# The low parts of 124 weight blocks: an accumulating transfer onto the negated rounded block instead of a VectorE difference

## The chip, the cores and the metric

The kernel runs on one core of one Trainium2 chip. The metric is device time in microseconds (us) of one execution on that core; lower is better. Engines are named as in the profile: PE is TensorE, DVE is VectorE, ACT is ScalarE, POOL is GpSimd, SP is SyncE, which issues the DMA transfers of the kernel before.

## The reference

One layer of a hybrid decoder is computed for 512 prompt tokens and 8 x 4 sample tokens, which share the weights. Cut to what matters here:

```
z   = rmsnorm(x) @ w_in                      # 1024 -> 9736: mixers a, b, c and the merge gates
y_a = (B * dwconv3(C * x_a)) @ w_out_a
y_b = silu(layernorm(dwconv31(...))) @ w_out_b
y_c = (sigmoid(o) * mlstm(q, k, v, ig, fg)) @ w_out_c      # 4 heads, chunks of 128
x  += (sig(g_a)*y_a + sig(g_b)*y_b + sig(g_c)*y_c) @ w_o
mk, mv = split(rmsnorm(mem) @ w_xkv)         # 256 memory tokens
x  += cross_attn(rmsnorm(x) @ w_xq, mk, mv) @ w_xo
x  += (silu(gate) * up) @ w_ffn_out          # gate, up = split(rmsnorm(x) @ w_ffn_in)
y   = rmsnorm(x)
```

All of it is float32, and every matrix product is wanted at nearly float32 accuracy.

## The kernel before

**Products in three passes.** Every operand of a product is held as two tiles: a high part, which is the float32 value rounded to the matmul format (fp32r), and a low part, which is the value minus its high part. A product is the sum of high x high, high x low and low x high. `PASSES` gives the order for each slice of 128 rows: the weight's high part with the activation's high part, then with its low part, and then the weight's low part with the activation's high part. With two halves of 272 tokens that is six matmuls for each slice; the weight's low part is first read by the fifth.

**Weight blocks.** PE's order is written by hand; the other engines' orders are made by a scheduler from the program's order and priorities. All weights are cut into blocks, and `order` is the list of them in the order in which PE uses them: `("in", j)` of `w_in`, `("v", ..)` and `("k", j)` of the memory's projection, `("oc"/"oa"/"ob", j)` of the mixers' output projections, `("o", j)`, `("xq", j)`, `("xo", j, half)`, `("fi", f, i)` of the first five feed-forward pairs, and others (`s..`, `fo`) later. A block is mostly 128 x 1024 numbers: eight slices, 48 matmuls of 272 columns, or 24 of 256 columns for the memory blocks. `oa`, `ob` and `xo` blocks are 128 x 512: 24 matmuls.

`w_emit` prepares a block: a DMA on SP's queue brings it into a raw tile `wr` (four of them), and `split` makes the two parts in a tile `w`: ACT writes the high part by a copy (`w<-wr` on ACT), then DVE writes raw minus high (`w<-wr,w` on DVE). There are **three** tiles `w` for all blocks. So the high part of a block can only be written when PE has ended with the block whose tile it takes; `wget` emits blocks two to four ahead. From then on the block has the time until PE comes to it.

**Stages.** Up to 46 us: the start, with the first two query blocks and two key blocks of head 0. 46 to 162 us: blocks of head 0 mixed with the sixteen memory blocks; here the block of output gate 0 spreads over 41 us and keeps one of the three `w` tiles, so the memory blocks turn over in two. 162 to 398 us: heads 1 to 3. 398 to 567 us: merge of mixer c and the inputs of mixer a, 1024-wide blocks one after the other. 567 to 712 us: the merges with `oa` and `ob`, where 1024-wide and 512-wide blocks alternate. 712 to 915 us: `o`, cross-attention with `xq` and `xo`. 915 to 983 us: the first five feed-forward pairs, two `fi` blocks each. After 983 us: the other pairs, which use another scheme (`s_emit`), and the final norm.

At the start POOL raises `small` (the mean squares of x) to the power -0.5 (`rms_pow`); PE's transposes in the middle of block `("in", 28)` wait for it.

Of the kernel before, what the change touches and what calls it, by code (L numbers as in the profile page):

```python
# [11 lines left out]
AF = mybir.ActivationFunctionType  # L12
# [23 lines left out]
def layer(ctx: ExitStack, tc: tile.TileContext, a):  # L36
    nc = tc.nc
# [27 lines left out]
    def nm(s):  # L65
        cnt[0] += 1
        return f"{s}_{cnt[0]}"
# [26 lines left out]
    def TTo(out, x, y, op):  # L94
        nc.vector.tensor_tensor(out=out, in0=x, in1=y, op=op)  # L95
# [7 lines left out]
    def STT(out, x, s, y, op0, op1):  # L103
        nc.vector.scalar_tensor_tensor(out=out, in0=x, scalar=s, in1=y, op0=op0, op1=op1)  # L104

    def ACT(out, x, f, **kw):
        nc.scalar.activation(out, x, f, **kw)  # L107
# [4 lines left out]
    def split(hi, lo, src, scale=None):  # L112
        if scale is None:
            ACT(hi, src, AF.Copy)
            TTo(lo, src, hi.bitcast(F32), ALU.subtract)
        else:
            ACT(hi, src, AF.Copy, scale=scale)
            STT(lo, src, scale, hi.bitcast(F32), ALU.mult, ALU.subtract)
# [4 lines left out]
    MULT, ADD, SUB, MAX, MIN = ALU.mult, ALU.add, ALU.subtract, ALU.max, ALU.min  # L123
# [22 lines left out]
    for h in range(NH):  # L146
        for base in (20, 28, 36, 44):
            for d in range(2):
                order += [("in", base + 2 * h + d)]
                if base == 44 and h == 0 or h == 1 and base < 36:  # L150
                    n = (1, 7)[d] if h == 0 else 2
# [36 lines left out]
    def w_emit(key, parts=1):  # L188

        if key[0][0] == "s":  # L190
            with tc.high_priority(PRIO):
                return s_emit(*key)
        if key[0] == "fo":
            return fo_emit(key)
        if key[0] == "v":
            src, n = a["w_v"][key[1], key[2]], 1024
        elif key[0] == "xo":
            n = 512
            src = a["w_xo"][key[1]][:, key[2] * n:(key[2] + 1) * n]
        elif key[0] == "fi":  # L200
            n = 1024
            src = a["w_fi"][key[1]][:, key[2] * n:(key[2] + 1) * n]
        else:
            src = a[src_of[key[0]]][key[1]]
            n = src.shape[-1]
        raw = sb.tile([P, 1024], F32, tag="wr", name=nm("wr"), bufs=4)
        w = sb.tile([P, 2, 1024], F32R, tag="w", name=nm("w"), bufs=3)
        wt[key] = w

        def part(i):  # L210
            c = slice(i * n // parts, (i + 1) * n // parts)
            with tc.high_priority(PRIO if parts == 1 and key not in (("in", 28), ("in", 29)) else 0):
                nc.sync.dma_start(out=raw[:, c], in_=src[:, c])
                split(w[:, 0, c], w[:, 1, c], raw[:, c])
        if parts == 1:
            part(0)
        return part

    def fo_emit(key):

        n = key[3] * P
        with tc.high_priority(PRIO):
            if n > 512:
                raw = sb.tile([P, 1024], F32, tag="wr", name=nm("wr"), bufs=4)
            else:
                raw = sb.tile([P, 512], F32, tag="sraw", name=nm("fr"), bufs=5)
            nc.sync.dma_start(out=raw[:, :n], in_=a["w_ffn_out"][key[1]][:, key[2] * P:key[2] * P + n])
            if n > 512:
                w = sb.tile([P, 2, 1024], F32R, tag="w", name=nm("w"), bufs=3)
            elif key in order[-6:]:  # L230
                w = act_t([P, 2, 512])
            else:
                w = sb.tile([P, 2, 512], F32R, tag="spair", name=nm("fw"), bufs=2)
            split(w[:, 0, :n], w[:, 1, :n], raw[:, :n])
        wt[key] = w
# [3 lines left out]
    def s_emit(part, f):  # L239

        if part == "sA":
            r = [sb.tile([P, 1024], F32, tag="wr", name=nm("wr"), bufs=4) for _ in range(2)]
            for i in range(2):
                nc.sync.dma_start(out=r[i], in_=a["w_fi"][f][:, i * 1024:(i + 1) * 1024])
            sraw_[f] = r
        r1, r2 = sraw_[f]
        if part in ("sA", "sC", "sE"):
            src = {"sA": r1[:, 0:512], "sC": r2[:, 0:512], "sE": r1[:, 512:]}[part]
            if f == NSTD and part != "sE":
                w = sb.tile([P, 2, 512], F32R, tag="spair", name=nm("fw"), bufs=2)  # L250
            else:
                w = act_t([P, 2, 512])
        else:
            w = sb.tile([P, 2, 1024], F32R, tag="w", name=nm("w"), bufs=3)
            if part == "sB":
                src = sb.tile([P, 1024], F32, tag="wr", name=nm("wr"), bufs=4)
                TTo(src.rearrange("p (a n) -> p a n", a=2), r1.rearrange("p (a n) -> p a n", a=2),
                    r2[:, 512:].rearrange("p (a n) -> p a n", a=1).to_broadcast([P, 2, 512]), ADD)
                TTo(r2[:, 512:], src[:, 512:], r1[:, 0:512], ADD)
            else:  # L260
                src = r2
                TTo(r2[:, 0:512], r2[:, 0:512], r2[:, 512:], ADD)
        split(w[:, 0, :], w[:, 1, :], src)
        wt[(part, f)] = w
# [800 lines left out]
    for c in range(4):  # L1065
# [13 lines left out]
        for j in range(3):  # L1079
            w = vec[:, V_AW + c * 3 + j:V_AW + c * 3 + j + 1]  # L1080
# [462 lines left out]
    parts = (slice(NP // 2, T), slice(0, NP // 2))  # L1543
# [183 lines left out]
```

## Time and profile before

| | |
|---|---|
| time, median of 3 runs (lowest to highest) | 1311.14 us (1310.72 to 1311.30) |
| the profiled execution's own time | 1310.35 us |
| its span, first to last instruction | 1308.3 us |
| PE busy | 1287.3 us, 98% of the span, 10160 matmuls |
| DVE busy | 887.5 us, 68% |
| ACT busy | 593.2 us, 45% |
| POOL busy | 40.9 us, 3% |
| DMA, mean share of 16 engines | 40.1% |

The profiled execution lies 0.8 us under the median, and 2.05 us of its time lie outside the span. Of the 1308.3 us PE is idle for 21.0. An engine that is not the one waited for may be idle, or busier, at no cost; what counts is which wait ends last in a stage.

### The profile page before, as it was taken

The page shows a single profiled execution, that of the slowest core. Times are in us where ns is not written, and L with a number is a line of the kernel's source. Part 1 is how long each engine was busy: PE and PEld are TensorE (multiplying, and loading weights), DVE is VectorE, ACT ScalarE, POOL GpSimd, SP SyncE. Part 2 cuts the span into 40 slices and gives each one's busy share as a digit, 9 for nine tenths or more (in the row PEclk, how much of TensorE's full clock was granted, in tenths as well). Part 3 has the DMA queues.
Part 4 walks back from the last instruction along what each step waited for, and adds up shares of the span by engine and source line. Part 5 has one row for each costly group of instructions (what it writes and reads, how often), then busy time and mean ns, then how long its engine had stood idle before and what let it go on. Part 6 is the DMA issues. An engine that isn't in the chain of part 4 may idle for free.

```text
span 1308.3 us, 24794 instructions
## 1 busy us (share of the span) xinstructions
PE 1287.3 (98%) x10160; PEld 1272.2 (97%) x10160; DVE 887.5 (68%) x1487; ACT 593.2 (45%) x1046; POOL 40.9 (3%) x117
## 2 busy tenths in 40 slices
PE   9899999999999999999999999999999999999997
PEld 9899999999999999999999999999999999999997
DVE  7955665655497859976444557886787667777746
ACT  6845545554433222226332446765544444444433
POOL 1000010010010000000000000000000000000000
PEclk9989999999999999999999999999999999999999
DMA  7355644434465333432334224664323323333212
GB/s 263 102 173 172 193 131 141 122 113 148 116 153 165 91 88 83 82 75 88 88 125 148 81 90 149 204 189 145 94 76 111 88 93 109 92 95 95 80 41 69
DMA packets 83265, 155.68 MB, mean 119 GB/s; under 512 B 25124, under 2 KB 33700, under 8 KB 83152
## 3 DMA queue, kind: packets, MB, share of 16 engines
q1 hardware_dynamic: 83152, 154.10, 40.1%
q8 instruction: 80, 1.31, 0.4%
q14 instruction: 33, 0.27, 0.1%
HBM read 137.54 MB, written 16.52 MB: 118 GB/s over the span
## 4 chain that ended last, share of the span: by engine, by line
PE 89%; DVE 5%; DMA 3%; issue 2%; ACT 2%; SPq 0%; POOL 0%; DVEq 0%; POOLq 0%; ACTq 0%
PE mm L110 60%; PE s L110 14%; PE sy L1475 8%; PE sz L1475 4%; PE sx L1475 2%; DVE f L95 1%; DMA out_sct<-ct 1%; DVE w L95 1%; DVE f L104 1%; ACT act L107 0%; DMA kr<-in_vc 0%; ACT w L107 0%; DMA f<-kscr 0%; DVE act L95 0%; DMA lt<-in_xT 0%
## 5 line engine op out<-in xcount | busy, mean ns | idle before, releaser
L110 PE MATMUL mm<-act,w 128*128 128x272 f32 x6336 | 837.8, 289 | 1.5 <-ACT f L107 0.9
L110 PEld LDWEIGHTS mm<-act,w 128*128 128x128 f32 x6336 | 809.5, 189 | 4.4 <-ACT f L107 1.1
L107 ACT ACTIVATE w<-wr 128x1024 fp32r<-128x1024 f32 (+2 forms) x202 | 196.6, 975 | 392.1 <-PE mm L110 228.9
L95 DVE TENSOR_TENSOR w<-wr,w 128x1024 fp32r<-128x1024 f32 (+2 forms) x202 | 225.5, 1117 | 144.3 <-ACT w L107 143.6
L104 DVE SCALAR_TENSOR_TENSOR f<-act,const,f 128x512 f32<-128x512 f32 (+1 forms) x136 | 96.5, 719 | 2.4
L95 DVE TENSOR_TENSOR lt<-mm,lt 128x544 f32<-128x544 f32 x56 | 40.4, 722 | 55.6 <-PE mm L110 55.4
L110 PE MATMUL mm<-act,fw 128*128 128x272 f32 x576 | 76.2, 288 | 0.0
L110 PEld LDWEIGHTS mm<-act,fw 128*128 128x128 f32 x576 | 73.9, 188 | 0.0
L107 ACT ACTIVATE act<-f 128x544 fp32r<-128x544 f32 (+3 forms) x75 | 44.3, 600 | 47.1 <-DVE f L95 40.8
L110 PE MATMUL s<-act,act 128*128 128x256 f32 (+4 forms) x408 | 62.9, 302 | 1.3 <-DVE act L95 0.8
L95 DVE TENSOR_TENSOR act<-f,act 128x544 fp32r<-128x544 f32 (+3 forms) x75 | 48.4, 653 | 22.1 <-ACT act L107 21.9
L95 DVE TENSOR_TENSOR f<-f,f 128x544 f32<-128x544 f32 (+4 forms) x78 | 51.3, 659 | 14.4 <-ACT f L107 13.1
L110 PEld LDWEIGHTS s<-act,act 128*128 128x128 f32 (+1 forms) x408 | 55.0, 184 | 4.4 <-DVE act L95 1.1
L1475 PE MATMUL sy<-bt,w 128*128 128x272 f32 x408 | 56.9, 288 | 0.6 <-ACT f L107 0.6
L1475 PEld LDWEIGHTS sy<-bt,w 128*128 128x128 f32 x408 | 53.4, 188 | 0.8 <-ACT f L107 0.8
L104 DVE SCALAR_TENSOR_TENSOR ct<-ct,wbc,s 128x258 f32<-128x258 f32 x64 | 28.7, 479 | 26.4 <-PE s L110 26.4
L107 ACT ACTIVATE f<-sy 128x272 f32<-128x272 f32 x51 | 19.8, 391 | 39.6 <-PE sy L1475 39.6
L95 DVE TENSOR_TENSOR wr<-wr,wr 128x1024 f32<-128x1024 f32 (+1 forms) x34 | 32.4, 954 | 5.4 <-DMA wr<-in_w_fi 4.9
L95 DVE TENSOR_TENSOR f<-mm,f 128x544 f32<-128x544 f32 (+1 forms) x29 | 20.7, 721 | 22.5 <-PE mm L110 20.4
L107 ACT ACTIVATE fw<-fr 128x512 fp32r<-128x512 f32 x26 | 16.4, 632 | 42.9 <-PE mm L110 39.0
L107 ACT ACTIVATE f<-mm 128x544 f32<-128x544 f32 (+1 forms) x50 | 30.6, 612 | 7.2 <-PE mm L110 7.0
L95 DVE TENSOR_TENSOR xpair<-kr,xpair 128x512 fp32r<-128x512 f32 x46 | 30.7, 682 | 3.5 <-ACT xpair L107 3.4
(238 smaller groups left out, 1406.3 us busy)
## 6 DMA issues: line engine op xcount, KB each, us to landing
wr<-in_w_in SPq DMA_DIRECT2D x74, 512.0 KB, 3.7
wr<-in_w_fi SPq DMA_DIRECT2D x44, 512.0 KB, 3.6
ct<-in_ctn SPq DMA_DIRECT2D x32, 258.0 KB, 3.1
out_sct<-ct SPq DMA_DIRECT2D x32, 258.0 KB, 3.8
kr<-in_ktc SPq DMA_DIRECT2D x32, 256.0 KB, 3.2
kr<-in_vc SPq DMA_DIRECT2D x32, 256.0 KB, 3.3
fr<-in_w_ffn_out SPq DMA_DIRECT2D x32, 256.0 KB, 2.7
lt<-in_xT SPq DMA_DIRECT2D x16, 272.0 KB, 3.9
```

The lines of the kernel that those rows point to most:

```text
L95: nc.vector.tensor_tensor(out=out, in0=x, in1=y, op=op)
L104: nc.vector.scalar_tensor_tensor(out=out, in0=x, scalar=s, in1=y, op0=op0, op1=op1)
L107: nc.scalar.activation(out, x, f, **kw)
L110: nc.tensor.matmul(out, lhsT=l, rhs=r, start=start, stop=stop)
L1475: nc.tensor.matmul(ps, lhsT=w[:, wi, c + k * P:c + (k + 1) * P], rhs=x(k, ai), start=first and k == 0 and n == 0, stop=k == 3 and n == 2, ...
```

## The change

For the 1024-wide blocks that `w_emit` loads whole (124 of them), ACT makes the high part as before, and then a second copy of the raw tile with scale -1 into the low half of `w`, which gives the negated rounded block. A DMA issued from POOL then reads the block a second time from memory and adds it onto that half, so that raw minus high stands there. DVE's difference is gone. The first two blocks (in two parts) and the 512-wide blocks keep `split`; so do the blocks that `fo_emit` and `s_emit` prepare.

```diff
@@ -211,7 +211,12 @@
             c = slice(i * n // parts, (i + 1) * n // parts)
             with tc.high_priority(PRIO if parts == 1 and key not in (("in", 28), ("in", 29)) else 0):
                 nc.sync.dma_start(out=raw[:, c], in_=src[:, c])
-                split(w[:, 0, c], w[:, 1, c], raw[:, c])
+                if parts == 1 and n == 1024:
+                    ACT(w[:, 0, c], raw[:, c], AF.Copy)
+                    ACT(w[:, 1, c], raw[:, c], AF.Copy, scale=-1.0)
+                    nc.gpsimd.dma_start(out=w[:, 1, c], in_=src[:, c], accum_op=ADD)
+                else:
+                    split(w[:, 0, c], w[:, 1, c], raw[:, c])
         if parts == 1:
             part(0)
         return part
```

PE's order and its instructions stay as they are. Lines after 219 stand five lines lower. Three places of the orders follow.

POOL from the rms of x on, before: `small_315` and `small_853` are the powers for x and for the memory, `f_98_675` a cleared tile of the gates, `km_..` a masked key of the sample tokens.

```order
L381 ISA
L381 TENSOR_TENSOR small_315<-small_314,const_67 128x5
L121 MEMSET f_98_675 68x544
L381 TENSOR_TENSOR small_853<-small_852,const_67 128x2
L874 TENSOR_SCALAR km_1424<-ks_1280,ph_157 96x256
```

The same place after: `w_162` is block ("in", 28), `w_299` is ("in", 36), `w_168` is ("in", 29), `w_390` is ("in", 37), `w_575`, `w_800` and `w_846` are memory blocks.

```order
L217 DMA w_162<-in_w_in 128x1024
L217 DMA w_299<-in_w_in 128x1024
L386 ISA
L386 TENSOR_TENSOR small_318<-small_317,const_67 128x5
L217 DMA w_168<-in_w_in 128x1024
L217 DMA w_390<-in_w_in 128x1024
L217 DMA w_478<-in_w_in 128x1024
L217 DMA w_575<-in_w_v 128x1024
L217 DMA w_720<-in_w_in 128x1024
L217 DMA w_800<-in_w_v 128x1024
L386 TENSOR_TENSOR small_862<-small_861,const_67 128x2
L121 MEMSET f_98_681 68x544
```

The transfer of block ("in", 29), the second key block of head 0, stands behind the power of x on POOL, and that of ("in", 36) ahead of it.

ACT among the memory blocks, before: `w_865` to `w_944` are high parts of memory blocks, `f_98_675`, `wir` and `ph_696` belong to the gates, `f_135` and `f_145` take the memory's values out of PSUM.

```order
L107 ACTIVATE w_865<-wr_864 128x1024
L107 ACTIVATE f_98_675<-f_98_675,const_690 4x512
L107 ACTIVATE f_98_675<-dl_693 4x32
L107 ACTIVATE wir_700<-wir_700 4x32
L107 ACTIVATE f_135_881<-s_123_797,const_856 128x256
L107 ACTIVATE ph_696<-wir_700 4x32
L107 ACTIVATE f_136_897<-s_124_798,const_856 128x256
L107 ACTIVATE w_902<-wr_901 128x1024
L107 ACTIVATE const_941<-s_141_938 128x256
L107 ACTIVATE f_145_960<-s_139_906,const_856 128x256
L107 ACTIVATE w_944<-wr_943 128x1024
```

The same place after; a row with x2 is the high part and the negated copy, one behind the other.

```order
L107 ACTIVATE w_874<-wr_873 128x1024 x2
L107 ACTIVATE f_98_681<-f_98_681,const_696 4x512
L107 ACTIVATE w_912<-wr_911 128x1024
L107 ACTIVATE const_952<-s_141_949 128x256
L107 ACTIVATE w_912<-wr_911 128x1024
L107 ACTIVATE f_98_681<-dl_699 4x32
L107 ACTIVATE wir_706<-wir_706 4x32
L107 ACTIVATE f_136_907<-s_124_806,const_865 128x256
L107 ACTIVATE ph_702<-wir_706 4x32
L107 ACTIVATE f_145_972<-s_139_917,const_865 128x256
L107 ACTIVATE w_955<-wr_954 128x1024 x2
```

The negated copy stands right behind the high part, or one short copy later.

DVE around the memory's sum of squares (`lt`), before: `w_793` and `w_838` are low parts, the L634 row is a scan of the gates.

```order
L104 SCALAR_TENSOR_TENSOR f_94_667<-f_72_469,f_93_658 4x544
L95 TENSOR_TENSOR c_232_1552<-ct_1550,c_232_1552 128x516
L95 TENSOR_TENSOR lt_738<-lt_738,mr_758 128x512
L95 TENSOR_TENSOR w_793<-wr_792,w_793 128x1024
L634 SCALAR_TENSOR_TENSOR f_95_669<-f_96_670,f_94_667 4x544
L95 TENSOR_TENSOR w_838<-wr_837,w_838 128x1024
L104 SCALAR_TENSOR_TENSOR f_98_675<-f_71_468,const_453,f_95_669 4x544
L95 TENSOR_TENSOR lt_738<-lt_738 128x256
```

The same place after.

```order
L95 TENSOR_TENSOR c_232_1574<-ct_1572,c_232_1574 128x516
L95 TENSOR_TENSOR f_93_664<-f_93_664,f_91_662 4x544
L95 TENSOR_TENSOR lt_745<-lt_745,mr_765 128x512
L104 SCALAR_TENSOR_TENSOR f_94_673<-f_72_473,f_93_664 4x544
L95 TENSOR_TENSOR lt_745<-lt_745 128x256
L101 TENSOR_SCALAR small_861<-s_129_858 128x2
L639 SCALAR_TENSOR_TENSOR f_95_675<-f_96_676,f_94_673 4x544
```

The two low parts are gone, and the last sum of the memory's squares stands ahead of the scan.

## Rows read from the trace of the kernel before

**Rows 1.** The page's head and part 1: busy us, share of the span, instructions.
```profile
span 1308.3 us, 24794 instructions
...
PE 1287.3 (98%) x10160; PEld 1272.2 (97%) x10160; DVE 887.5 (68%) x1487; ACT 593.2 (45%) x1046; POOL 40.9 (3%) x117
```

**Rows 2.** The page's part 4: the chain that ended last, by engine.
```profile
PE 89%; DVE 5%; DMA 3%; issue 2%; ACT 2%; SPq 0%; POOL 0%; DVEq 0%; POOLq 0%; ACTq 0%
```

**Rows 3.** PE's waits, longest first: total us, times, longest us.
```profile
PE s L110 <- DVE lt L95: 5.3, 1, 5.3
PE s L110 <- DVE f L95: 1.7, 2, 1.5
```

**Rows 4.** Stages: us, busy us (instructions) of PE, PEld, DVE, ACT, POOL; PEclk, DMA.
```profile
46.00:162.00 116.00, 109.24 (x859) 107.35 (x859) 71.62 (x129) 68.90 (x124) 4.90 (x9) 0.96 0.57 170
...
398.00:567.00 169.00, 169.00 (x1346) 169.00 (x1347) 140.72 (x209) 41.07 (x52) 0.41 (x4) 1.00 0.38 96
```

**Rows 5.** Groups by form, ACT's and DVE's: xcount | busy us, mean ns | idle before.
```profile
L107 ACT ACTIVATE w<-wr 128x1024 fp32r<-128x1024 f32 x158 | 167.3, 1060 | 312.3 <-PE mm L110 169.1 <-issue 84.3 <-PE s L110 18.4
...
L95 DVE TENSOR_TENSOR w<-wr,w 128x1024 fp32r<-128x1024 f32 x158 | 193.2, 1223 | 101.2 <-ACT w L107 100.6
```

**Rows 6.** The timeline at the start: start us, us, engine, line, instruction.
```profile
17.44 1.04 ACT L107 ACTIVATE w<-wr 128x1024 fp32r<-128x1024 f32 x1
...
19.18 1.22 DVE L95 TENSOR_TENSOR w<-wr,w 128x1024 fp32r<-128x1024 f32 x1
19.37 2.01 ACT L107 ACTIVATE w<-wr 128x1024 fp32r<-128x1024 f32 x2 [0.89 <-PE mm L110]
...
22.77 2.11 POOL L381 TENSOR_TENSOR small<-small,const 128x5 f32<-128x5 f32 x1 [18.62 <-DVE small L101]
```

**Rows 7.** DMA issues: count, KB each, median us from issue to landing; all block loads.
```profile
wr<-in_w_fi SPq DMA_DIRECT2D x44, 512.0 KB, 3.6
...
wr<-in_w_xo SPq DMA_DIRECT2D x16, 256.0 KB, 2.6
...
DMA to landing us min/median/max: 2.5/3.6/7.6
```

**Rows 8.** POOL's groups by form.
```profile
L381 POOL TENSOR_TENSOR small<-small,const 128x5 f32<-128x5 f32 x2 | 3.3, 1638 | 87.5 <-DVE small L101 87.5
...
L121 POOL MEMSET vt<- 128x1 f32 x16 | 1.4, 98 | 0.7
```

**Rows 9.** The chain in order of time, merge stages: start us, us, what.
```profile
397.99 187.02 PE mm L110 x1488
```

**Rows 10.** The timeline among the memory blocks: ACT's high parts, PE's next use.
```profile
74.63 1.06 ACT L107 ACTIVATE w<-wr 128x1024 fp32r<-128x1024 f32 x1 [2.07 <-issue]
...
78.14 3.11 PE L110 MATMUL s<-w,act 128*128 128x256 f32 x24
...
113.75 1.06 ACT L107 ACTIVATE w<-wr 128x1024 fp32r<-128x1024 f32 x1 [0.96 <-PE s L110]
...
118.86 3.03 PE L110 MATMUL s<-w,act 128*128 128x256 f32 x24
...
143.30 1.06 ACT L107 ACTIVATE w<-wr 128x1024 fp32r<-128x1024 f32 x1 [0.87 <-PE mm L110]
...
147.91 3.02 PE L110 MATMUL s<-act,w 128*128 128x256 f32 x24
```

**Rows 11.** Block ("o", 1): ACT's high part in the timeline.
```profile
709.65 1.06 ACT L107 ACTIVATE w<-wr 128x1024 fp32r<-128x1024 f32 x1 [3.83 <-PE mm L110]
```

**Rows 12.** Block ("o", 1): PE's start on it, in the chain.
```profile
713.47 2.65 PE mm L110 x19
```

**Rows 13.** The timeline at the first feed-forward pair: high parts of its blocks.
```profile
915.17 1.06 ACT L107 ACTIVATE w<-wr 128x1024 fp32r<-128x1024 f32 x1 [1.00 <-ACT f L107]
...
921.20 1.06 ACT L107 ACTIVATE w<-wr 128x1024 fp32r<-128x1024 f32 x1 [0.41 <-ACT f L107]
```

**Rows 14.** The page's part 3: queue, packets, MB, share of 16 engines' span.
```profile
q1 hardware_dynamic: 83152, 154.10, 40.1%
```

## The prediction

> **What bounds the kernel now.** I read the page's busy times first, then the chain that ended last, PE's waits, and stage by stage the timeline of the weight tiles. PE is busy for 1287.3 of 1308.3 us [rows 1] and has 89% of the chain [rows 2]; the chain runs through the merge as one piece of 1488 matmuls in 187.02 us, 0.1257 us each [rows 9]. So the change cannot gain much: all that PE stands idle is 21.0 us, and its two largest waits for DVE are 5.3 and 1.7 us [rows 3]. DVE, which is relieved, is busiest in the merge with 140.7 of 169 us, and there PE does not wait at all [rows 4]. What PE has everywhere is a supply of blocks through three tiles. The question is therefore not how much work DVE loses, but how long a block now takes from a free tile to a finished low part, against the matmuls that PE has to do until it wants it.
>
> **The change: what is removed and added.** Removed are 124 differences of 1.22 us on DVE [rows 5], 152 us of an engine that bounds no stage: worth nothing by itself. Added are 124 negated copies on ACT. Two copies one behind the other take 2.01 us [rows 6], so the second costs 0.95: 118 us more, which brings ACT from 593 to about 711 of 1308 us, 54%. Added are 124 transfers from POOL, 65 MB read again; the queue before took 40.1% of the DMA engines for 154 MB [rows 14], so 65 to 130 MB more (one or two readings) makes it 57 to 74%: no bound on the mean.
>
> **The new turnaround.** Before, the low part stood at about 1.3 us after the end of the high copy, where DVE was free (ACT's mean and DVE's 1.22 us in rows 5). After, it stands there after T = 0.95 (negated copy) + L, where L runs from that copy's end to the landing of the accumulating transfer. No row of before shows such a transfer. Below, L is bounded by the plain load of as many bytes, 3.6 us from issue to landing [rows 7]. Above: the longest plain load took 7.6; a second reading of 512 KB, priced by the step from 256 to 512 KB (3.6 - 2.6 = 1.0), adds 2.0; and POOL must write what it issues, between 0.1 us (its smallest rows) and 2.1 (the power of x) [rows 6, 8]: 11.7 together. I take median values: 3.6 + 2.0 for reading and adding onto what stands in the tile + 1.1 for POOL = **L 6.7, T 7.7**, nearest to the plain load because the bytes and rows are the same. It is an estimate, and the whole forecast hangs on it.
>
> The Trainium skill, "DMA: Bandwidth & Descriptors", section "Anatomy of one DMA — SWDGE (gpsimd) path", gives 2.0 us plus bytes at 436 GB/s for a transfer issued from GpSimd, and "Collectives: The Full Stack", in the section on the bandwidth ceiling, says that an add in the DMA engine reads two sources; an estimate from both pages is 4.4 us for this one. With that as L the sum below would be some 15 us instead of 46; no run here shows either yet.
>
> **Where T is too long.** A block's budget is the time from the end of its high copy to PE's first read of the low part: the matmuls between the tile's release and that read, at 0.1257 us, less about 1.16 for release and copy.
> - Merge, 1024-wide blocks in a row: two blocks of 48 matmuls and four more, 12.6 - 1.2 = 11.4 us. T fits, 3.7 to spare. In heads 1 to 3 side work makes the blocks longer still. Cost nothing, and the cover is these two blocks.
> - `oa` and `ob`: one block of 48 and one of 24, 9.6 - 1.2 = 8.4. It just fits; 0.3 us for one block that is released late.
> - Start: block ("in", 28) has its high part at 17.44 + 1.04 = 18.48, and PE took the low part as soon as DVE wrote it, at 20.40 [rows 6]. T ends at 26.2: **5.7 us**. Behind it on PE are the sums of squares and the power of x, so those go 5.7 later too.
> - Then POOL's order: the transfer of ("in", 29) stands behind the power, which ended at 24.88 [rows 6]. 24.9 + 6.7 = 31.6, against a first low read at about 29.3, 48 matmuls, ten small ones and the transposes behind 20.4: **2.3 us**. All later POOL work waits behind transfers only until they are issued.
> - Memory blocks, two tiles in turn: copy done at 75.69, read at 78.14 + 0.25 = 78.4: budget 2.7, short 5.0. The next block's tile came free before this stall, so it has 5 us more and fits; the one after it starts over and is short 4.8. On through the stage, read in the same way: 3.0; 3.4 (budget 4.3, copy done at 114.81, read at 119.1); 2.6; 1.2 (copy done 144.36, read 148.2, budget 3.8, 2.6 of the shortage of 3.9 paid by the stall just before); small ones 0.4 [rows 10]. **20.4 us.**
> - ("o", 1): copy done at 710.71 [rows 11], read at 713.47 + 0.5 [rows 12]: 4.4; the second block of `xq`, in the same pattern, 1.4. **5.8 us.**
> - `fi`: the first block's copy ends at 916.23 and PE comes to the block two `xo` blocks later, when the copy at 921.20 starts, its low part at 921.5 [rows 13]: budget 5.2, short 2.45. In each later pair the second block has again 48 matmuls only: 1.6 and three times 2.45. **11.4 us.**
>
> Sum: 5.7 + 2.3 + 20.4 + 0.3 + 5.8 + 11.4 = 45.9 us.
>
> Against it stands DVE's relief. The wait of 5.3 us for the memory's sum of squares [rows 3] should lose the two differences and the scan that stood ahead, some 3 us; but PE then comes 3 us sooner to memory blocks whose parts do not come sooner, so I take nothing for it. Evacuations on ACT may stand up to 0.95 us behind a negated copy; with 124 copies and some fifty blocks before the merge that is between 0 and some 12 us, and I take 0, because ACT is busy for 69 of 116 us even among the memory blocks [rows 4]. PE's granted clock was 0.96 there, with its waits of over 5 us; I count no further loss by the clock.
>
> 1310.35 (the profiled execution) + 45.9 = 1356.2; it lies 0.8 under the median of the runs, so **1357 us**, 3.5% slower.
>
> **Rivals.**
> - Short landing: the second reading is hidden beside the first and POOL's writing beside both, L 3.6 to 4.7. For it: same rows and bytes as the plain load. Against: reading and adding must come before writing. At 3.6 only the start (2.6), three or four memory blocks (4.6) and ("o", 1) (1.3) are short: 8.5 us, 1320; at 4.7 some 17, 1329. The skill's figure above falls in it.
> - Long landing: the accumulation runs at a fraction of the plain rate, or waits behind the raw loads, which share the engines (0.57 busy among the memory blocks [rows 4]). At L 9 the seventeen places are each 2.3 us worse (39), the blocks of `oa` and `ob` fall short by up to 1.6 each, as far as a stall doesn't pay for the next (13), and blocks between the short ones join (8 to 10): 106, so 1418. At 10, with merge blocks near their 11.4, some 140.
> - ACT as the new wait: evacuations and high copies queue behind negated copies, which adds up to 12 us to either; it is in the range, not a case of its own.
> - Faster: DVE's relief wins. It takes DVE's whole 7.0 us of the two waits and some smaller ones, 10 in all, and decides only where the shortages are below that: from L under about 3.8, the lower bound. At 3.6 with all 10 given back the time is 1310.
>
> **Chances.** L from 4.7 to 8, the forecast, 0.58 (17 to 78 us: 1328 to 1389, its own range). Short landing 0.14, long landing 0.22, relief wins or evens out 0.06. A time under 1322 needs the best half of the short case, and one over 1430 L above 9.4: about 1 in 10 each, so 1322 to 1430. A difference of 0.2% (2.6 us) is about what a measurement of this kernel can tell from no change; only the last case reaches it: faster 0.03, same 0.04, slower 0.93.
>
> **What would show it.** In the profile after: DVE near 736 us and ACT near 711; POOL rows for 124 transfers on a queue of their own, with landings; PE's waits naming POOL's DMA into `w` as releaser, in total 40 to 50 us, at about 20, 78, 85, 94, 119, 714 and in five places from 921 on; PE without a gap from 398 to 567. Each stretch's lengthening by these amounts shows its term right. It is wrong if the landings are not between 4.7 and 8 us, if merge stages show waits (then L is over 10), if the waits name ACT rather than a DMA, or if PE's granted clock falls in the stalled stretches.

## The result, and the profile after

The changed kernel takes 1438.17 us (median of 4 runs, 1436.12 to 1444.88) against 1310.93 for the kernel before in the same runs: 1.0983 times as long, 95% interval 1.0964 to 1.1003. The forecast was 1357 with a range to 1430. The direction was right and most of the places were right; the size was not: 127 us instead of 46.

The page's head and part 1 of the kernel after, which answer to [rows 1], and of part 3 the two large queues, SP's and POOL's (packets, MB, share of 16 engines' span), which answer to [rows 14]:

```profile
span 1437.9 us, 25071 instructions
...
PE 1328.4 (92%) x10160; PEld 1303.8 (91%) x10160; DVE 752.8 (52%) x1363; ACT 706.7 (49%) x1170; POOL 148.8 (10%) x241
...
q1 hardware_dynamic: 83152, 154.10, 36.9%
q0 software_dynamic: 17856, 65.02, 25.2%
```

The span grew by 129.6 us, and the first lines split it in two. PE stands idle for 1437.9 - 1328.4 = 109.5 us, 88.5 more than before; and PE's own time for the same 10160 matmuls is 41.1 us longer. ACT's total came near the forecast (706.7 us against 711), DVE's lies 17 us above it (752.8 against 736); neither is a bound.

PE's waits in the kernel after, longest first (total us, times, longest us), which answer to [rows 3]:

```profile
PE mm L110 <- DMA w<-in_w_in: 24.8, 15, 7.3
PE s L110 <- DMA w<-in_w_v: 17.8, 4, 6.6
PE mm L110 <- DMA w<-in_w_fi: 16.7, 5, 3.9
PE s L110 <- DMA w<-in_w_k: 13.0, 4, 6.3
PE mm L110 <- DMA w<-in_w_o: 6.7, 3, 4.9
PE s L914 <- DVE num L99: 6.6, 1, 6.6
PE mm L110 <- DMA w<-in_w_xq: 2.7, 1, 2.7
```

Six rows name a transfer into `w`: 81.7 us. They are the waits that the prediction named, but for 12.0 us of the first row: 5.1 of these lie in the merge, forecast at nothing, and 6.9 in the stage of `oa` and `ob`, forecast at 0.3. The row with `num` is another thing, and the experiments come back to it.

The issues on POOL by line (count, KB, median us from issue to landing), and the landings of all transfers into `w`, which answer to [rows 7]:

```profile
w<-in_w_in POOLq DMA_DIRECT2D x74, 512.0 KB, 7.8
w<-in_w_fi POOLq DMA_DIRECT2D x10, 512.0 KB, 7.7
...
DMA to landing us min/median/max: 5.4/7.8/11.1
```

The timeline at the second pair of `fi` blocks (start us, us, engine, line, instruction) shows one turnaround:

```profile
1039.52 2.01 ACT L107 ACTIVATE w<-wr 128x1024 fp32r<-128x1024 f32 x2 [12.38 <-PE mm L110]
...
1041.82 0.92 POOL L217 DMA_DIRECT2D w<-in_w_fi  x1 [4.15 <-ACT w L107]
...
1049.32 8.89 PE L110 MATMUL mm<-act,w 128*128 128x272 f32 x47 [2.83 <-DMA w<-in_w_fi]
```

The two copies end at 1041.53; POOL issues 0.29 us later; PE starts when the low part has landed, 7.8 us after the copies. And then 47 matmuls take 8.89 us, where 47 x 0.1257 [rows 9] would be 5.9. That is the second part of the loss. The stages (us, busy us of each engine with counts, then the granted clock, the DMA share and GB/s), which answer to [rows 4]:

```profile
56.00:216.00 160.00, 120.51 (x861) 116.36 (x860) 46.13 (x106) 89.89 (x146) 24.67 (x32) 0.88 0.79 192
...
638.00:793.00 155.00, 148.05 (x1160) 145.86 (x1158) 57.81 (x90) 72.39 (x94) 13.83 (x16) 1.00 0.64 150
...
1017.00:1112.00 95.00, 78.27 (x544) 76.92 (x543) 45.00 (x77) 41.81 (x56) 9.97 (x12) 0.89 0.52 117
```

The `fi` stage in the kernel before, in the same columns:

```profile
915.00:983.00 68.00, 68.00 (x543) 67.76 (x542) 55.60 (x87) 33.03 (x46) 1.22 (x2) 1.00 0.28 85
```

In the `fi` stage 544 matmuls take 78.3 us of PE's own time at a granted clock of 0.89; before it was 68 us for 543 at 1.00. Among the memory blocks the clock is 0.88, before 0.96 [rows 4]. Where the waits are short (`oa` and `ob`, 638 to 793, none over 1.5 us) it stays 1.00.

PE issues the same matmuls in the same order in both kernels, so each stage can be measured between the same two matmuls. In us, stages by their bounds before:

| stage | forecast | measured | of it idle | PE's own time |
|---|---|---|---|---|
| 0 to 46, start | 8.0 | 10.2 | 7.0 | 3.2 |
| 46 to 162, memory blocks | 20.4 | 43.7 | 32.7 | 11.0 |
| 162 to 398 | 0 | 9.9 | 6.5 | 3.4 |
| 398 to 567, merge | 0 | 7.7 | 5.1 | 2.6 |
| 567 to 712, oa and ob | 0.3 | 9.7 | 7.0 | 2.7 |
| 712 to 915, o, xq, xo | 5.8 | 21.4 | 13.5 | 7.9 |
| 915 to 983, fi | 11.4 | 26.9 | 16.7 | 10.2 |
| from 983 | 0 | 0.1 | 0.0 | 0.1 |

### The profile page after: what moved, and what is told of

Read it like the earlier page. It is cut to its first block, busy times and chain, and to the rows that moved or that the text cites. A ratio compares the mean times of both kernels' runs of the same rounds, so it can differ in the third digit from the quotient of the medians.

```text
span 1437.9 us, 25071 instructions
## 1 busy us (share of the span) xinstructions
PE 1328.4 (92%) x10160; PEld 1303.8 (91%) x10160; DVE 752.8 (52%) x1363; ACT 706.7 (49%) x1170; POOL 148.8 (10%) x241
## 3 DMA queue, kind: packets, MB, share of 16 engines
q0 software_dynamic: 17856, 65.02, 25.2%
## 4 chain that ended last, share of the span: by engine, by line
PE 72%; DMA 18%; issue 5%; ACT 3%; DVE 2%; POOL 0%; SPq 0%; POOLq 0%; DVEq 0%; ACTq 0%
PE mm L110 47%; PE s L110 12%; DMA w<-in_w_in 8%; PE sy L1480 7%; PE sz L1480 3%; DMA w<-in_w_fi 3%; DMA w<-in_w_k 2%; DMA w<-in_w_v 2%; ACT w L107 2%; PE sx L1480 2%; DMA w<-in_w_o 1%; ACT f L107 1%; DMA w<-in_w_xq 1%; DMA f<-kscr 0%; ACT act L107 0%
## 5 line engine op out<-in xcount | busy, mean ns | idle before, releaser
L110 PE MATMUL mm<-act,w 128*128 128x272 f32 x6336 | 863.5, 294 | 53.4 <-DMA w<-in_w_in 24.8
L110 PEld LDWEIGHTS mm<-act,w 128*128 128x128 f32 x6336 | 829.4, 193 | 62.1 <-DMA w<-in_w_in 29.0
L107 ACT ACTIVATE w<-wr 128x1024 fp32r<-128x1024 f32 (+2 forms) x326 | 314.0, 1000 | 412.6 <-issue 200.9
L95 DVE TENSOR_TENSOR w<-wr,w 128x512 fp32r<-128x512 f32 (+2 forms) x78 | 73.9, 949 | 66.6 <-ACT w L107 66.5
L217 POOL DMA_DIRECT2D w<-in_w_in x74 | 64.8, 875 | 424.2 <-ACT w L107 369.9
L110 PE MATMUL s<-act,act 128*128 128x256 f32 (+4 forms) x408 | 66.4, 310 | 3.9 <-ACT act L107 2.7
L110 PE MATMUL s<-w,act 128*128 128x256 f32 x192 | 29.8, 317 | 18.3 <-DMA w<-in_w_v 17.8
L110 PEld LDWEIGHTS s<-w,act 128*128 128x128 f32 x192 | 28.1, 225 | 19.3 <-DMA w<-in_w_v 18.6
L110 PE MATMUL s<-act,w 128*128 128x256 f32 x192 | 31.6, 330 | 13.0 <-DMA w<-in_w_k 13.0
L110 PEld LDWEIGHTS s<-act,w 128*128 128x128 f32 x192 | 29.9, 237 | 14.0 <-DMA w<-in_w_k 13.8
```

The costliest lines, as they stand in the source:

```text
L110: nc.tensor.matmul(out, lhsT=l, rhs=r, start=start, stop=stop)
L217: nc.gpsimd.dma_start(out=w[:, 1, c], in_=src[:, c], accum_op=ADD)
```

## The experiments

The theory under test: time is lost where the turnaround T is longer than the matmuls that cover it, and behind the longer waits once more by PE's clock. Its rivals: a cost of each transfer wherever it stands (shared DMA engines), and ACT's 118 us more as the wait. First a table of all, then one by one. Idle and PE's own time are the span minus PE's busy time, and PE's busy time, of the profiled execution, less those of [rows 1].

| kernel | median us | ratio, 95% interval | added idle | added PE time | issue to landing, median |
|---|---|---|---|---|---|
| after | 1438.17 | 1.0983 (1.0964 to 1.1003) | 88.5 | 41.1 | 7.8 |
| e1 plain transfer | 1366.02 | 1.0423 (1.0391 to 1.0455) | 37.9 | 21.5 | 5.0 |
| e2 quarter | 1350.75 | 1.0306 (1.0286 to 1.0327) | 24.3 | 16.0 | 4.6 |
| e3 halves | 1408.19 | 1.0743 (1.0706 to 1.0779) | 69.4 | 34.2 | 6.8 |
| e4 covered, 52 | 1328.77 | 1.0142 (1.0125 to 1.0159) | 11.5 | 5.0 | 7.9 |
| e5 negated on DVE | 1396.30 | 1.0641 (1.0609 to 1.0673) | 63.2 | 24.6 | 7.7 (w_in) |
| e6 low last | 1388.65 | 1.0594 (1.0566 to 1.0623) | 53.5 | 27.7 | 7.9 (w_in) |
| e7 before, low last | 1315.51 | 1.0046 (1.0025 to 1.0067) | 3.4 | 1.9 | |
| e8 ACT's copy alone | 1321.97 | 1.0084 (1.0062 to 1.0107) | 7.9 | 6.6 | |
| e9 fi alone | 1337.44 | 1.0204 (1.0191 to 1.0218) | 16.3 | 11.1 | 7.8 |
| e10 delay of 8 | 1331.89 | 1.0160 (1.0144 to 1.0175) | 14.2 | 7.9 | |
| e11 delay of 6 | 1317.72 | 1.0055 (1.0040 to 1.0070) | 5.5 | 4.7 | |
| e12 sums first | 1304.67 | 0.9953 (0.9941 to 0.9966) | -3.8 | -1.6 | |
| e13 covered, 41 | 1314.86 | 1.0037 (1.0024 to 1.0051) | 2.2 | 2.7 | 7.9 |

**e1: the same transfer without the adding.**

```diff
-                    nc.gpsimd.dma_start(out=w[:, 1, c], in_=src[:, c], accum_op=ADD)
+                    nc.gpsimd.dma_start(out=w[:, 1, c], in_=src[:, c])
```

> The changed kernel, but POOL's transfer only writes the block over the low half and adds nothing (so the low parts are wrong: they hold the whole block). Same queue, same bytes, same order. Theory A, the adding is what is slow: the time from the negated copy's end to landing falls from a mean of 8.35 to between 4.5 and 5.5 us, PE idles some 15 to 30 us instead of 109.5, and the time is 1330 to 1355. Theory B, the way over POOL is what is slow whatever the transfer does: 7.5 us or more to landing, time above 1400.

Part 3 of its page, POOL's queue, and its landings into `w`:

```profile
q0 software_dynamic: 17856, 65.02, 13.9%
...
DMA to landing us min/median/max: 3.8/5.0/9.7
```

The landing falls from 7.8 to 5.0 us, so the adding costs 2.8; the time, 1366, lies 11 us above what theory A gave, and far under theory B's. PE's idle time, 58.9 us, is above the 15 to 30 of theory A too. On the engines the price can be read too: 25.2% of 1437.9 us over 124 transfers are 2.9 us of all sixteen engines for one that adds, 13.9% of 1367.7 are 1.5 for one that writes. Adding doubles the engines' time, as a second reading would. The Trainium skill, "Collectives: The Full Stack", section on the bandwidth ceiling, says that an add in the DMA engine reads two sources, and the trace agrees. The other page of the Trainium skill that the prediction named, "DMA: Bandwidth & Descriptors", section "Anatomy of one DMA — SWDGE (gpsimd) path", makes, as an estimate from its figures, 3.2 us for this plain transfer; here the shortest took 3.8 and the median 5.0, and the measurement decides.

**e2: only a quarter of the columns added.**

```diff
-                    nc.gpsimd.dma_start(out=w[:, 1, c], in_=src[:, c], accum_op=ADD)
+                    nc.gpsimd.dma_start(out=w[:, 1, :256], in_=src[:, :256], accum_op=ADD)
```

> The changed kernel, but the accumulating transfer covers only the first 256 of 1024 columns (the other low parts stay the negated block, so they are wrong). PE's first low read still waits for it. Theory A, the bytes are what is slow: landing about 3 to 4 us after the negated copy's end, time 1320 to 1335. Theory B, a fixed latency: 7 us or more, time above 1390. Between them (5 to 6.5 us, 1340 to 1375) both parts count, and the difference to 8.35 is the price of 384 KB.

4.6 us from issue to landing, some 4.9 from the copy's end: between the two theories, the time inside the band for both parts counting and the landing just under it. The 384 KB less save 3.2 us. Even this small transfer makes T 0.95 + 4.9 = 5.8 us, over the 2.7 to 5.2 of the tightest budgets.

**e3: two transfers of half the columns.**

```diff
-                    nc.gpsimd.dma_start(out=w[:, 1, c], in_=src[:, c], accum_op=ADD)
+                    for q in (slice(0, 512), slice(512, 1024)):
+                        nc.gpsimd.dma_start(out=w[:, 1, q], in_=src[:, q], accum_op=ADD)
```

> The changed kernel with the accumulating transfer cut into two of 512 columns, so that PE's first slices wait for the first half alone. Theory A, bytes: the first half lands about 5 us after the negated copy, time near 1340. Theory B, fixed latency: some 7 us, time 1380 to 1400. Rival C, the two pieces share the engines and land together, and POOL writes twice as many rows: both at 8.5 to 9.5 us, time 1440 to 1460.

1408, 30 us better than whole blocks, and landings of 6.8 us: nearest to theory B, a little worse. POOL is busy for 258.9 us instead of 148.8, so the second piece is issued later than a whole block would be; that the two pieces also slow each other on the DMA engines is likely, but not shown.

**e4: only blocks with long budgets.**

```diff
-                if parts == 1 and n == 1024:
+                if parts == 1 and n == 1024 and (key[0] == "oc" or key[0] == "in" and (
+                        key[1] < 20 or key[1] >= 68 or key[1] < 52 and (key[1] - 20) % 8 >= 4)):
```

> Accumulating transfers only for 52 blocks with long budgets: w_in of heads 2 and 3 and of the merges up to 567 us in the profile before, and oc; the other 72 keep VectorE's difference. Theory T, only the turnaround against the matmuls between counts: the landings stay near 8 us, PE does not wait for them, and the time is that of the kernel before, 1309 to 1314. Rival, each transfer, each negated copy or the second reading costs something wherever it stands: 52/124 of 127 us, so about 1364.

18 us slower: neither. The memory blocks, `o`, `xq` and `fi` are as before, as theory T has it; but two things are new. PE waits 5.7 us for four late landings (up to 11.4 us), and 6.6 us for `num`, the numerators of the last head. The timeline ahead of that wait:

```profile
385.00 0.38 SPq L888 DMA_DIRECT2D out_sct<-ct  x1
...
389.19 0.34 SPq L1207 DMA_DIRECT2D kr<-in_ktc  x1
...
393.88 0.63 ACT L107 ACTIVATE k<-kr 128x512 fp32r<-128x512 f32 x1 [6.03 <-DMA kr<-in_ktc]
...
394.55 0.69 DVE L95 TENSOR_TENSOR k<-kr,k 128x512 fp32r<-128x512 f32 x1 [5.51 <-ACT k L107]
...
395.16 0.16 DVE L95 TENSOR_TENSOR small<-ssq,small 128x5 f32<-128x5 f32 x1
...
402.86 1.17 PE L915 MATMUL s<-const,num 128*128 128x128 f32 x4 [6.58 <-DVE num L99]
```

Cached keys (`kr`) are late on SP's queue, ACT stands 6.0 us before them, DVE 5.5 behind ACT, and behind DVE's `k` stands the small arithmetic (`small`) that scales `num`. SP issued such loads only after a write of the state (`out_sct`) had landed. Its waits for that from 370 to 420 us (total us, times, longest), first in the kernel before, then in e4:

```profile
SPq L1201 <- DMA out_sct<-ct: 18.4, 5, 5.7
```

```profile
SPq L1207 <- DMA out_sct<-ct: 24.4, 5, 9.4
```

From 370 to 400 us the DMA engines are busy for 0.90 of the time in e4, 0.67 before. So it looks as if transfers that PE never waits for slowed the state's writes, these held back the loads, and two engines wait for the loads in their order. That POOL's transfers began it is not yet shown by this; e13 asks it.

**e5: the negated block made by DVE, beside ACT's copy.**

```diff
-                    ACT(w[:, 1, c], raw[:, c], AF.Copy, scale=-1.0)
+                    TS(w[:, 1, c], raw[:, c], -1.0, MULT)
```

> The changed kernel with the negated block written by VectorE from the raw tile, beside ACT's high copy and no longer behind it. Theory T (turnaround against matmuls): up to 0.95 us less in each of the places that decide; PE's added idle time falls from 88 to some 60 us, the clock's share from 41 to some 27, time 1390 to 1405. Rival, ACT's queue is the new wait (118 us of copies moved away from it): more than T gives, under 1385. Rival, the wait is only that of the transfers' landings in a busy memory: no change, 1430 to 1440.

1396, inside theory T's 1390 to 1405. 0.95 us less of turnaround is worth 42 us: 25 of idle time and 17 of PE's own. That there are so many places to gain from is what e5 shows: the waits that name a transfer into `w` fall from 81.7 us in 32 waits to 54.0 in 22. ACT also has 112 us less of work (595.0 busy against 706.7); a gain of its own from that does not show, as the time stays inside theory T's band, but e5 changes both at once and does not measure them apart.

**e6 and e7: PE reads the low part last; and the same order in the kernel before.** In `block`, and in the same way in `two_blocks`, the memory blocks and `fi`:

```diff
-        for k in range(nk):
-            mm_k(ps, w, acts, k, k == 0, k == nk - 1)
...
+        for i in range(3 * nk):
+            if i < 2 * nk and i % 2 == 0:
+                mm_k(ps, w, acts, i // 2, i == 0, False, PASSES[:2])
+            if i >= 2 * nk:
+                mm_k(ps, w, acts, i - 2 * nk, False, i == 3 * nk - 1, PASSES[2:])
```

> The changed kernel with PE's own order inside a block changed: all products with the high part first, those with the low part last, so that the first low read comes 28 matmuls (3.5 us) later in a wide block, 14 (1.8 us) in a memory block, 12 (1.5 us) in a fi pair; nothing else moves. Theory T: at the measured 8.35 us to landing 38 us of added idle time stay instead of 84, with the clock's share and some 10 us of late loads 1360 to 1380. Rival, contention of the transfers or ACT's load decides: above 1415, since neither is changed.

> The kernel before with the same order of PE's matmuls. Control for the run with the changed kernel: 1305 to 1312, since low parts were hardly ever waited for; it could save the small waits among the memory blocks, some 1 us.

e6 came to 1389, 50 us better than the changed kernel, and 9 above the band; e7 shows that the order itself costs 4.4 us here, which I had not expected, and which makes up half of that. Nothing about transfers or ACT was changed, so the rival's 1415 is out: the cover decides.

**e8: ACT's second copy alone.**

```diff
+                if parts == 1 and n == 1024:
+                    ACT(w[:, 1, c], raw[:, c], AF.Copy, scale=-1.0)
```

> The kernel before plus ACT's second copy alone: ACT writes the negated block into the low half, and VectorE's difference then writes over it; no transfer on POOL. Theory T: low parts 0.95 us later and ACT as busy as in the changed kernel, short of no budget but the tightest memory blocks: 1311 to 1317. Rival, ACT's 118 us more are a new wait in front of evacuations and high parts: 1320 to 1335.

11 us, at the lower edge of the rival and beyond theory T: the prediction named 0 to some 12 and took 0. The waits are PE's for `lt` (8.1 instead of 5.3) and small ones for evacuations. Every low part comes 0.95 us later here as well, so the 11 us are the price of both together.

**e9: the change for the ten `fi` blocks alone.**

```diff
-                if parts == 1 and n == 1024:
+                if parts == 1 and key[0] == "fi":
```

> The change for the ten w_fi blocks alone; the other 114 wide blocks keep VectorE's difference. Theory T: landings about as long as in the changed kernel (7 to 8 us from issue), five waits of 2.8 to 3.9 us at the second block of each pair, and PE slower by its clock behind each: this stage longer by 23 to 28 us, nothing else changed, 1333 to 1339. Rival, the long landings come from 65 MB more on the DMA engines in all: with 5 MB they fall towards 5.5 us, the waits to under 1 us, and the time is 1312 to 1318.

PE's first wait and the landings into `w` of this kernel:

```profile
PE mm L110 <- DMA w<-in_w_fi: 16.3, 5, 4.0
...
DMA to landing us min/median/max: 6.7/7.8/9.4
```

With 5 MB instead of 65 the landing is as long, 7.8 us, the five waits are 16.3 instead of 16.7 us, and the stage is 26.2 us longer against 26.9. So the long landing does not come from the other accumulating transfers, and the stage's loss is made in the stage. SP's loads of raw blocks still run beside these ten; what they add to a landing was not tested.

**e10 and e11: the same lateness without any transfer.** The low part of the second `fi` block of each pair is held back by clearings on POOL, eight or six:

```diff
+                if key[0] == "fi" and key[2] == 1:
+                    for _ in range(8):
+                        MS(w[:, 1, :], 0.0)
                 split(w[:, 0, c], w[:, 1, c], raw[:, c])
```

> The kernel before, and no transfer added: the low part of the second w_fi block of each of the five pairs is held back by eight clearings of its half on POOL (1.15 us each by the 128x1152 rows), so it stands about 9.4 us after the high copy. Theory T with the clock: five waits of 3 to 4 us, PE's own time in the stage longer by some 10 us as behind the transfers: 1333 to 1341. Rival, transfers into SBUF and not idle time slow PE's matmuls: the waits alone, 1326 to 1330.

> The same with six clearings: the low part stands some 7.1 us after the high copy, five waits of about 1.3 to 1.8 us. Theory, the clock falls only behind the longer waits (as the stage of oa and ob in the changed kernel, with waits up to 1.5 us at a granted clock of 1.00): 1318 to 1322, PE's own time in the stage longer by 2 us at most. Rival, the clock's loss goes with the idle time whatever its length (0.47 us for each us): some 4 us more, 1321 to 1326.

The `fi` stage of e10 in the columns of the stages above, then PE in the timeline of e10, and after it of e11 (start us, us, instruction, idle before it):

```profile
915.00:1004.00 89.00, 75.13 (x542) 73.79 (x541) 56.29 (x86) 33.19 (x46) 39.44 (x42) 0.92 0.21 65
```

```profile
945.67 12.33 PE L110 MATMUL mm<-act,w 128*128 128x272 f32 x96 [2.15 <-DVE w L95]
960.94 13.85 PE L110 MATMUL mm<-act,w 128*128 128x272 f32 x96 [2.95 <-DVE w L95]
977.73 13.85 PE L110 MATMUL mm<-act,w 128*128 128x272 f32 x96 [2.94 <-DVE w L95]
```

```profile
942.29 12.32 PE L110 MATMUL mm<-act,w 128*128 128x272 f32 x96 [0.27 <-DVE w L95]
955.53 12.32 PE L110 MATMUL mm<-act,w 128*128 128x272 f32 x96 [0.92 <-DVE w L95]
969.65 13.84 PE L110 MATMUL mm<-act,w 128*128 128x272 f32 x96 [1.80 <-DVE w L95]
```

The same 96 matmuls take 12.3 us behind one wait and 13.85 behind another: 1.5 us more, at a granted clock that was in part 1.2 instead of 2.4 GHz (0.92 in the stage). No transfer writes late here, so the idle time itself does it. A clearing took 0.96 us, not the 1.15 assumed, so the waits of e10 were 13.9 us in all, under 3 each, and its stage 21.2 us longer (13.9 idle, 7.3 PE's own): 1331.89 is just under the theory's band and above the rival's. In e11 waits of 0.9 cost nothing more, and one of 1.80 did, while 2.15 in e10 did not: the length of a wait alone does not decide, and what else does stays open. Neither of the two rules that e11 was to tell apart holds as I wrote it, and its 1317.72 lies just under the bands of both.

**e12: the relief of DVE by itself.** In `mem_in` of the kernel before:

```diff
-                TTo(macc, macc, m, ADD)
+                urgent(lambda: TTo(macc, macc, m, ADD))
...
-                TTo(macc[:, 0, :], macc[:, 0, :], macc[:, 1, :], ADD)
+                urgent(lambda: TTo(macc[:, 0, :], macc[:, 0, :], macc[:, 1, :], ADD))
```

> The kernel before with the memory's sums of squares ahead of the two differences and the scan on VectorE, as the relieved VectorE of the changed kernel had them; the differences come right behind. The relief as the prediction put it is worth some 3 us of the wait of 5.3: 1307 to 1309. Rival, PE only comes sooner to memory blocks that are not ready, and nothing is gained: 1310 to 1312.

PE's wait for the sums, and the stage of the memory blocks:

```profile
PE s L110 <- DVE lt L95: 1.1, 1, 1.1
...
46.00:157.00 111.00, 107.68 (x865) 105.18 (x864) 71.94 (x130) 69.52 (x125) 5.76 (x9) 1.00 0.59 177
```

1304.67, 6.4 us under the kernel before in the same runs (1311.08), more than either expectation: it beats both kernels. The wait went from 5.3 to 1.1, and the stage's clock from 0.96 to 1.00; PE's own time for the same matmuls is 2.3 us shorter there. It takes no transfer: only the order on DVE.

**e13: e4 less the eleven blocks beside the late loads.**

```diff
+                if parts == 1 and n == 1024 and (key[0] == "oc" and key[1] > 0 or key[0] == "in" and (
+                        key[1] < 12 or key[1] >= 70 or 20 <= key[1] < 52 and (key[1] - 20) % 8 >= 4)):
```

> As the run with 52 covered blocks, less the eleven whose transfers stood in the stretch from 320 to 420 us (four each of w_in 12 to 15 and 16 to 19, two more of w_in, the first oc), in which the state is written back and the cached keys are loaded on SP's queue; 41 blocks keep the accumulating transfer. Theory, the 18 us of that run came from transfers beside those loads (keys late, ACT and VectorE stuck behind them, PE's wait of 6.6 us for the head's numerators, its clock) and from two to four landings of over 10 us: the first goes, the landings late in the merge stay, 1311 to 1316. Rival, the transfers, copies and readings themselves cost wherever they stand: 41/52 of 18 us, 1325.

1314.86, as the first theory said. The wait for `num` is 0.7 us again, SP's longest wait for a write of the state is 5.6 us and the DMA share from 370 to 400 us 0.65, both as in the kernel before. Three waits for landings remain, 2.5 us. 41 transfers of 21 MB cost 5.3 us against the kernel before in the same runs (1309.54); the eleven taken away had cost some 13, as e4 lost 18.2. With each of the eleven its negated copy on ACT went too.

## Why the prediction was wrong in size

**The mechanism and most places were right.** The longest waits lie at the start, among the memory blocks, at ("o", 1), `xq` and the second `fi` block of each pair, they name POOL's transfer into `w`, and from 983 us on nothing changed. e6 and e10 change only the cover or the turnaround, e5 the turnaround and ACT's work, and the time follows. By the prediction's own signs it was wrong: its L lies over 8 us, the merge shows waits, and the clock fell. Its rival with a long landing, given 0.22, had the landing right.

**L was mis-sized: 6.7 us forecast, 8.35 measured** (mean of the 124: 0.43 from the negated copy's end to the issue, 7.93 from issue to landing). Both parts were short. In medians: plain load and POOL's writing, 3.6 + 1.1 = 4.7 forecast, 5.3 measured (0.29 to the issue, and 5.0 in e1, of which 0.54 is POOL's writing). Adding: 2.0 forecast from the plain price of 512 KB, 2.8 measured, 0.33 of it POOL's (0.87 for an issue that adds). That is 8.1; the long landings bring the mean to 8.35. The arithmetic on budgets itself held: between the prediction's own two points, 46 us at an L of 6.7 and 106 at 9, an L of 8.35 lies at some 89 us, against 81.7 in the rows that name the transfers. It also explains two of the stages forecast at nothing or nearly so: landings spread from 5.4 to 11.1 us. With 8.35 the turnaround is 9.3, over the budget of 8.4 of `oa` and `ob`; and in the merge, with 11.4, the three longest waits stand behind landings of 10.4, 11.1 and 11.1 us, where one value for all transfers fitted.

**The clock was left out: 0 forecast, most of 41 us measured.** Besides the size of L, the step that failed is "I count no further loss by the clock". The granted clock of 0.96 in [rows 4] stood on the one wait of over 5 us in that stage, and the prediction itself put five waits of 2.6 to 5.0 us into it and five into `fi`. Each such wait could have been priced from that row: 0.04 of 116 us, 4.6 at most. The clock records of the traces give the loss: of PE's busy time 75.8 us ran at 1.2 GHz in the changed kernel and 6.8 before, and half of the difference, 34.5 us, is what the lower level cost (9.9 of the 10.2 us in the `fi` stage, 9.3 of the 11.0 among the memory blocks). The Trainium skill, "TensorE: Matmul & The Clock Gate", section "HAM oscillation — how this bites in real kernels", describes this: waits for a DMA between groups of matmuls let the clock fall, and each group starts slow again. The granted 0.88 and 0.89 agree, and e10 shows the same with waits that are not for a DMA.

**ACT's copies: 0 taken, 11 us alone** (e8, with the later low parts). That in the changed kernel they are not a sum on top is argued: the waits are for the landings, and e5, which frees ACT, gains no more than 0.95 us of turnaround was forecast to give.

**"No bound on the mean" was right and not enough.** The DMA share was 0.79 among the memory blocks and 62% over the whole, yet eleven transfers beside the state's writes and the loads on SP's queue cost some 13 us by way of `num` and of landings over 10 us (e4 against e13). The 9.9 us in the stage from 162 to 398, forecast at nothing, are of this kind: 6.6 of them are the wait for `num`, and no wait there names a transfer into `w`. For the changed kernel only the likeness to e4 is shown: the same 6.6 us, and a longest wait of ACT for `kr` of 9.6 us in both, against 6.6 before.

**DVE's relief: taken as nothing.** The wait for `lt` did fall, to 1.1 us, and that stage still became 43.7 us longer; that the gain was given back in the next memory blocks, as the prediction said, is not shown apart. By itself the earlier sum is worth 6 us (e12).

What stays open: where the 6.6 us of PE's own time come from that the clock does not explain (2.7 of them arose in the stage of `oa` and `ob` at a clock of 1.00), and why reading the low parts last costs the kernel before 4.4 us. A fourth `w` tile, the plain remedy, was not tried.

## What to carry to other kernels

Price a step moved to DMA by its turnaround in the rings it feeds, not by the work it takes from an engine: here an engine with 30% to spare lost 1.2 us a block, and the block's path from the high copy to the low part grew from about 1.3 to 9.3 us. Budgets read from the trace (matmuls between a tile's release and the low part's first read) gave the right places; use the spread of the landing and not one value, and add a price for PE's clock behind each wait of a few us (here 34.5 us in all). Where a relieved engine is wanted early, try its order first: that was worth 6 us with nothing moved.

## What was not expected of the hardware

An accumulating transfer of 512 KB from memory into SBUF took 7.8 us from issue to landing, whether 65 MB or 5 MB went that way in all; without the adding 5.0, and 4.6 for 128 KB with it. It takes 2.9 us of all sixteen DMA engines, against 1.5 for a plain one. Beside such transfers a write of the state held SP for up to 9.4 us, against 5.7 without them. A wait of 1.80 us in one place cost PE 1.5 us of clock and one of 2.15 us in another place none.
